# First product of the key and value compression, as four products side by side in quarters of the array's columns

## The chip, the cores and the metric

The kernel runs on one core of one Trainium2 chip. A core has five engines with their own instruction streams: TensorE (PE in the profile; PEld is its loading of weights), VectorE (DVE), ScalarE (ACT), GpSimd (POOL) and SyncE (SP, which here only starts transfers). Each engine takes its instructions in the order in which the program holds them, and waits on semaphores for what the others make. The metric is the device time of one execution in microseconds (us); lower is better.

## The reference

One decoder layer for 256 tokens of width 1024, float32 throughout. The part that matters here is the compression of the keys and values of the "native sparse attention" heads, two key/value groups of 64 columns:

```python
CMP_LEN, CMP_STRIDE, CMP_HID = 32, 16, 256

def _compress(kraw, pe, w1, b1, w2):
    B, S, G, DH = kraw.shape
    ncb = (S - CMP_LEN) // CMP_STRIDE + 1                     # 15 blocks
    idx = jnp.arange(ncb)[:, None] * CMP_STRIDE + jnp.arange(CMP_LEN)[None, :]
    blk = kraw[:, idx] + pe[None, None, :, None, :]
    blk = blk.transpose(0, 1, 3, 2, 4).reshape(B, ncb, G, CMP_LEN * DH)
    return jax.nn.gelu(blk @ w1 + b1) @ w2
```

It runs once for the keys (after their rotation) and once for the values. Each kind has 15 blocks x 2 groups = 30 rows of 32 x 64 = 2048 numbers, multiplied with a matrix of 2048 x 256 (the first product), then a GELU, then 256 x 64. The compressed keys give one of three attention branches its scores, the compressed values its output. Around it stand, in this order: a normalization modulated by a condition vector, one large projection, the retention heads and the attention heads, an output projection, a second normalization, and a retrieval of experts by product keys (PEER) with two large weight tables.

## The kernel before

The program is written in stages; a scheduler then places every engine's instructions in an order of its own, so the order in the source is not the order on an engine. Where the text below says "the order", it is the order in the built program.

Up to about 183 us runs what the source calls the prefix: the condition columns ("ada"), norm 1, the projection blocks, rotations, `compress` for keys and for values, the retention scores (`S<-qrT,krT`, copied decayed to `sT`), eight attention units, the output projection and norm 2. The rest, to 1038 us, is PEER.

`compress(kv)` does, for one kind (`"k"` or `"v"`):
- products with `ident` bring `kn` (keys) or `vcn` (values) to 64 rows a half; VectorE adds the position terms and writes `blk`, 128 rows (two tokens of a block, 64 columns each) x 16 x 30.
- four loads of 128 x 4 x 256 weights (`praw`, 0.5 MB each, three buffers, `PRAW`), and sixteen products `praw` x `blk`: the weights of the array are a 128 x 30 piece of `blk`, the moving operand 128 x 256 of `praw`. All sixteen add up in one accumulation of 30 rows x 256 in a bank `O`. Each float32 product is two records in the trace.
- ScalarE copies the sums to `hn` (30 x 256), TensorE transposes them in two parts, and a chain of small VectorE steps with one ScalarE tanh makes the GELU: `cu`, `cw` four times, `hid`.
- for the keys: `hid` x `w2k` gives the compressed keys, copied to `kcT`. For the values: `hid` x `w2v`, `vc`, a product with `rep`, and `vblk`.

`compress("k")` is called, then `compress("v")`. The scores of the attention follow: `cmp_softmax(tt)` for a half `tt` of the tokens (scores `S<-kcT,qT`, small steps `cs_s`, `cs_m`, `cs_p`, and the transposed `cs_pT`), then for each of four pairs of heads `attn_unit`: scores `S<-keys,qT`, VectorE's maximum `a_mx`, ScalarE's exponentials `a_pr` with their sums `a_sm`, a scaling, transposes `T<-ident,a_pr` and the copy `a_pT`; and `attn_pv`: products of `a_pT` with `vs` and of `cs_pT` with `vblk` into one bank `O`, a group of heads in each half of the array's columns. `mixNH` and `mixNL` are the two float32r parts of the result. Scores use two banks `S`, transposes two banks `T`.

Between these stand fillers without a part in the chain: products C of a projection block (`half`, from weights that ScalarE and VectorE split into `H` and `L`), the splits of the output projection's weights (`woH`, `woL`), and VectorE's passes over `adaraw` (128 x 1024) with which later condition columns are summed. The retention's tail (`rv`, `sg`, `rn`) ends beside the attention. Calls of helpers are all recorded at line 80.

Of the kernel before, what the change touches and what calls it, by code (L numbers as in the profile page):

```python
# [24 lines left out]
F32 = mybir.dt.float32  # L25
# [6 lines left out]
ALU = mybir.AluOpType  # L32
# [4 lines left out]
P = 128  # L37
# [11 lines left out]
PRAW = 3  # L49
# [14 lines left out]
def build(tc, I, out, dbg=None, stop=None):  # L64
# [5 lines left out]
    class Ordered:  # L70
        """An engine whose instructions stay in program order while order["on"] has its name."""
# [82 lines left out]
    def rstd_of(pool, ss, n, inv, tag):  # L154
        """1/sqrt(ss * inv + eps), a square root and one Newton step."""
# [13 lines left out]
    def rstd_pair(pool, sa, sb, tag, between=lambda: None):  # L169
        """Two factors of 1/sqrt((sa + sb) / D + eps): a square root's inverse and one Newton step."""  # L170
# [15 lines left out]
    # ------------------------------------------------------------------ prefix  # L186
# [11 lines left out]
    def table(func, dep=None):  # L198
        """Has a function's table loaded before a chain needs it, once dep is there."""
        t = mk(pers, (P, 1), F32, "tinyo", bufs=2)  # L200
        S.activation(t, tiny if dep is None else dep, func, scale=0.0)
# [29 lines left out]
    # 2 silu(c) on every partition  # L231
# [36 lines left out]
    # norm 1: the product that transposes a row block scales it too  # L268
# [38 lines left out]
    # projection blocks A (q | kc ks kw vc) and B (rq | vs vw gate)  # L307
# [92 lines left out]
    def rope(dst, src, tab, tt, nh, dh, v=0):  # L400
        """dst (SBUF) = rotated src (PSUM), nh heads of dh."""
# [24 lines left out]
    def half(c, post, nf=0):  # L426
        """A projection block of 512 columns; post(i) after each of its four units."""
# [56 lines left out]

    rr = {}
# [23 lines left out]
    # NSA transposes  # L509
# [22 lines left out]
    # compressed keys and values  # L532
# [4 lines left out]
    def compress(kv):  # L537
        pe_t, b1_t, w2_t = cmpc[kv]
# [7 lines left out]
        blk = mk(wk, (P, 16, 2, 15), F32, "blk", bufs=1)  # L546
        for s in range(2):
            rows = slice(s * 64, (s + 1) * 64)
            bv = b[rows, :].rearrange("p (g t) -> p g t", g=2)
            for g in range(2):  # L550
                src = bv[:, g, s:s + 1]
                src = bass.AP(tensor=src.tensor, offset=src.offset, ap=[list(src.ap[0]), [2, 16], [16, 15]])
                V.tensor_tensor(blk[rows, :, g, :], src, pe_t[rows, :, None].to_broadcast([64, 16, 15]), op=ALU.add)
        b = bank("O")
        for i in range(4):
            key = ("w" + kv, i)
            load(key, I["w" + kv + "1"][:, i * 4:i * 4 + 4, :], (P, 4, 256))
            r, _ = raws.pop(key)
            for q in range(4):
                mm(b[:30, :256], blk[:, i * 4 + q].rearrange("p a b -> p (a b)"), r[:, q * 256:(q + 1) * 256],  # L560
                   i == 0 and q == 0, i == 3 and q == 3)
        hn = mk(wk, (32, 256), F32, "hn", bufs=1)
        S.activation(hn[:30, :], b[:30, :256], AF.Copy)
        b = bank("O")
        for ch in range(2):
# [755 lines left out]
```

## Time and profile before

| | |
|---|---|
| time, three runs | 1039.51, 1039.74, 1041.83 us (median 1039.74) |
| span of the profiled execution | 1037.9 us (no other time of this execution is given) |
| TensorE busy over the span | 1009.2 us (97%) |
| VectorE, ScalarE, GpSimd busy | 760.4 us (73%), 606.8 us (58%), 61.5 us (6%) |
| first product of `praw` to last | 70.4 to 95.5 us |
| eight attention units | about 85 to 145 us |

The profile is one execution with the time of every instruction. A busy time counts an instruction's own time; matmul ends are modelled, and successive matmuls overlap, so their distance is read from their starts. Idle time of an engine is listed with what ended it. The rows that are used stand in a section of their own below.

### The profile page before, as it was taken

How to read it: one execution, taken by the hardware profiler on the slowest of the kernel's cores; microseconds unless marked ns; L12 is line 12 of the kernel's file. 1: busy time of each engine (PE TensorE's matmuls, PEld its weight loads, DVE VectorE, ACT ScalarE, POOL GpSimd, SP SyncE). 2: the span in 40 equal slices, each digit the busy share in tenths (PEclk: the TensorE clock that was granted, in tenths of full speed). 3: DMA queues.
4: the chain of work that ended last, by engine and by line, in shares of the span. 5: the costliest groups of instructions: out<-in, count | busy, mean ns of one | idle time of the engine just before them, and what ended most of it. 6: DMA issues, size and time to landing. Idle time of an engine off the chain costs nothing.

```text
span 1037.9 us, 17713 instructions
## 1 busy us (share of the span) xinstructions
PE 1009.2 (97%) x6580; PEld 902.1 (87%) x6582; DVE 760.4 (73%) x1653; ACT 606.8 (58%) x1244; POOL 61.5 (6%) x53
## 2 busy tenths in 40 slices
PE   7999999999998889999999999999999999999995
PEld 6876687999998889999999999988888888888884
DVE  7988888899778786667777777665955556565665
ACT  7544884555436357777777777645445555545453
POOL 1040000000331310000000000000000000000001
PEclk9999999999999999999999999999999999999998
DMA  9998753546555444444444444567976666666661
GB/s 367 352 350 335 244 181 136 168 152 183 168 149 174 144 152 135 151 147 143 148 142 144 143 143 143 156 230 231 317 234 193 197 190 214 190 199 188 198 189 57
DMA packets 56184, 199.19 MB, mean 192 GB/s; under 512 B 7305, under 2 KB 7585, under 8 KB 55713
## 3 DMA queue, kind: packets, MB, share of 16 engines
q1 hardware_dynamic: 55200, 193.59, 58.3%
q0 software_dynamic: 752, 4.20, 1.1%
q8 instruction: 51, 0.84, 0.3%
q14 instruction: 37, 0.30, 0.1%
q10 hardware_dynamic: 144, 0.26, 0.1%
HBM read 195.92 MB, written 2.11 MB: 191 GB/s over the span
## 4 chain that ended last, share of the span: by engine, by line
PE 84%; DVE 9%; POOL 3%; ACT 1%; issue 1%; DMA 0%; SPq 0%; DVEq 0%; POOLq 0%; ACTq 0%
PE acc L80 54%; PE dn L80 9%; PE w L80 7%; PE C L80 5%; PE O L80 4%; POOL oe L946 3%; PE S L80 3%; PE T L80 2%; DVE ev L80 2%; DVE L L80 2%; DVE oh L80 1%; DVE tp L80 1%; DVE VL L80 1%; DVE adaraw L80 0%; DMA xn<-in_x_dram 0%
## 5 line engine op out<-in xcount | busy, mean ns | idle before, releaser
L80 DVE TENSOR_TENSOR L<-raw,H 128x1024 fp32r<-128x1024 f32 x284 | 346.4, 1221 | 119.5 <-ACT H L80 114.9
L80 ACT ACTIVATE H<-raw 128x1024 fp32r<-128x1024 f32 x284 | 300.0, 1058 | 172.4 <-PE acc L80 132.6
L80 PE MATMUL acc<-H,a 128*128 128x512 f32 (+1 forms) x1030 | 315.9, 388 | 0.0
L80 PE MATMUL acc<-hH,H 128*128 128x256 f32 x800 | 230.8, 289 | 0.0
L80 PE MATMUL acc<-hH,L 128*128 128x256 f32 x800 | 226.6, 283 | 3.3 <-DVE L L80 3.3
L80 PEld LDWEIGHTS acc<-H,a 128*128 128x128 f32 x1030 | 193.0, 188 | 39.9
L80 PE MATMUL acc<-hL,H 128*128 128x256 f32 x800 | 226.6, 283 | 0.0
L80 PE MATMUL acc<-L,a 128*128 128x512 f32 (+1 forms) x515 | 199.7, 388 | 0.0
L80 PEld LDWEIGHTS acc<-hH,L 128*128 128x128 f32 x800 | 152.9, 191 | 4.1 <-DVE L L80 4.1
L80 PEld LDWEIGHTS acc<-hH,H 128*128 128x128 f32 x800 | 153.5, 192 | 0.1
L80 PEld LDWEIGHTS acc<-hL,H 128*128 128x128 f32 x800 | 153.2, 192 | 0.2 <-DVE hL L80 0.2
L80 PEld LDWEIGHTS acc<-L,a 128*128 128x128 f32 x515 | 96.7, 188 | 19.7
L80 ACT ACTIVATE ow<-o,VL 128x128 f16<-128x128 f16 x256 | 104.5, 578 | 5.2 <-DVE o L80 5.2
L80 PE MATMUL dn<-hH,L 128*128 128x256 f32 x352 | 99.8, 283 | 4.4 <-DVE L L80 4.4
L80 PE MATMUL dn<-hH,H 128*128 128x256 f32 x352 | 101.5, 288 | 0.4 <-ACT H L80 0.4
L80 PE MATMUL dn<-hL,H 128*128 128x256 f32 x352 | 99.6, 283 | 0.0
L80 PEld LDWEIGHTS dn<-hH,L 128*128 128x128 f32 x352 | 67.3, 191 | 5.0 <-DVE L L80 5.0
L80 PE MATMUL w<-ow,o 128*128 128x128 f16 x512 | 71.0, 296 | 0.0
L80 PEld LDWEIGHTS dn<-hH,H 128*128 128x128 f32 x352 | 67.6, 192 | 0.6 <-ACT H L80 0.6
L80 PEld LDWEIGHTS dn<-hL,H 128*128 128x128 f32 x352 | 67.4, 192 | 0.0
L80 PEld LDWEIGHTS <-o 128*128 128x128 f16 x512 | 51.9, 118 | 3.4
L80 DVE TENSOR_TENSOR ow<-o,VL 128x512 f16<-128x512 f16 x64 | 26.9, 420 | 36.9 <-PE w L80 36.9
(333 smaller groups left out, 1213.5 us busy)
## 6 DMA issues: line engine op xcount, KB each, us to landing
raw<-in_down_dram SPq DMA_DIRECT2D x128, 512.0 KB, 3.6
raw<-in_up_dram SPq DMA_DIRECT2D x128, 512.0 KB, 3.7
adaraw<-in_wadaT_dram SPq DMA_DIRECT2D x40, 512.0 KB, 8.0
raw<-in_wq_dram SPq DMA_DIRECT2D x16, 512.0 KB, 3.7
raw<-in_win_C_dram SPq DMA_DIRECT2D x12, 512.0 KB, 5.2
rawA<-in_win_A_dram SPq DMA_DIRECT2D x8, 512.0 KB, 9.6
raw<-in_wout_dram SPq DMA_DIRECT2D x8, 512.0 KB, 4.7
VL<-in_wadaT_dram SPq DMA_DIRECT2D x8, 512.0 KB, 4.6
```

The costliest lines, as they stand in the source:

```text
L80: i = fn(*a, **kw)
L946: G.tensor_tensor(oe, oh, cidx[:, p, :, None].to_broadcast([P, NCAND, 16]), op=ALU.mult)
```

## The change

The sixteen products of each kind become part of one pass for both kinds. A piece of `blk` is widened to 32 columns (two of them zero, from a memset), so that a quarter of the array's 128 columns holds it. The four quarters hold the even and the odd products of the keys and of the values; all four add up in one bank, 32 rows each. One copy of 128 x 256 takes the bank to `hn`. The even and odd sums of a kind are added when they are turned: instead of a transpose, a product with `sel4`, a 0/1 matrix that VectorE makes once from `ident`. The weights of both kinds are loaded in turn, with four buffers instead of three. Docstrings and comments are removed as well.

```diff
-PRAW = 3
+PRAW = 4
...
+    sel4 = mk(pe_, (P, 32), F32, "sel4")
+    V.tensor_reduce(sel4, ident.rearrange("p (a b) -> p b a", a=4), axis=AX.X, op=ALU.add)
...
-    def compress(kv):
-        pe_t, b1_t, w2_t = cmpc[kv]
+    def blocks(kv):
+
+        pe_t = cmpc[kv][0]
         b = bank("O")
...
-        blk = mk(wk, (P, 16, 2, 15), F32, "blk", bufs=1)
+        blk = mk(wk, (P, 16, 32), F32, "blk" + kv, bufs=1)
+        G.memset(blk, 0.0)
+        bl = blk[:, :, :30].rearrange("p a (g c) -> p a g c", g=2)
...
-                V.tensor_tensor(blk[rows, :, g, :], src, pe_t[rows, :, None].to_broadcast([64, 16, 15]), op=ALU.add)
+                V.tensor_tensor(bl[rows, :, g, :], src, pe_t[rows, :, None].to_broadcast([64, 16, 15]), op=ALU.add)
+        return blk
+
+    def compress_sums(blks):
+
         b = bank("O")
         for i in range(4):
-            key = ("w" + kv, i)
-            load(key, I["w" + kv + "1"][:, i * 4:i * 4 + 4, :], (P, 4, 256))
-            r, _ = raws.pop(key)
-            for q in range(4):
-                mm(b[:30, :256], blk[:, i * 4 + q].rearrange("p a b -> p (a b)"), r[:, q * 256:(q + 1) * 256],
-                   i == 0 and q == 0, i == 3 and q == 3)
-        hn = mk(wk, (32, 256), F32, "hn", bufs=1)
-        S.activation(hn[:30, :], b[:30, :256], AF.Copy)
+            rs = {}
+            for kv in "kv":
+                key = ("w" + kv, i)
+                load(key, I["w" + kv + "1"][:, i * 4:i * 4 + 4, :], (P, 4, 256))
+                rs[kv], _ = raws.pop(key)
+            for q2 in range(2):
+                for c, (kv, o) in enumerate((("k", 0), ("k", 1), ("v", 0), ("v", 1))):
+                    q = q2 * 2 + o
+                    PE.matmul(b[c * 32:(c + 1) * 32, :256], blks[kv][:, i * 4 + q], rs[kv][:, q * 256:(q + 1) * 256],
+                              start=i == 0 and q2 == 0, stop=i == 3 and q2 == 1, tile_position=(0, c * 32))
+        hn = mk(wk, (P, 256), F32, "hn", bufs=1)
+        S.activation(hn, b[:, :256], AF.Copy)
+        return hn
+
+    def compress(kv, hn):
+        pe_t, b1_t, w2_t = cmpc[kv]
         b = bank("O")
+        rows = slice(0, 64) if kv == "k" else slice(64, P)
         for ch in range(2):
-            PE.transpose(b[:, ch * 32:ch * 32 + 30], hn[:30, ch * P:(ch + 1) * P], ident[:30, :30])
+            mm(b[:, ch * 32:ch * 32 + 30], hn[rows, ch * P:(ch + 1) * P], sel4[rows, :30], True, True)
...
-    compress("k")
-    compress("v")
+    blks = {kv: blocks(kv) for kv in "kv"}
+    hn2 = compress_sums(blks)
+    compress("k", hn2)
+    compress("v", hn2)
```

The scheduler places the new instructions, and with them others of the prefix: on every engine the order differs from that of before up to the end of the attention and the output projection, and is the same from there on. Three places follow, each of before and then of the changed kernel, as the built programs hold them (out<-in, shape of the output; x2 is two in a row; a number is a buffer's).

TensorE, in the middle of the first sums (`O<-praw,blk`; S are retention scores, C fillers), before:

```order
L80 MATMUL O_789<-praw_790,blk_784 30x256 x3
L80 MATMUL O_789<-praw_796,blk_784 30x256 x4
L80 MATMUL O_789<-praw_802,blk_784 30x256 x4
L80 MATMUL S_913<-qrT_582,krT_583 128x256
L80 MATMUL O_789<-praw_808,blk_784 30x256 x4
L80 MATMUL S_913<-qrT_582,krT_583 128x128
L80 MATMUL S_918<-qrT_582,krT_583 128x256
L80 MATMUL O_816<-ident_66,hn_814 128x30 x2
```

and in the changed kernel, from the last load's products of both kinds to the key's `hid` and the value's turned sums:

```order
L80 MATMUL O_807<-praw_846,blkv_801 32x256 x2
L80 MATMUL O_807<-praw_844,blkk_786 32x256 x2
L80 MATMUL O_807<-praw_846,blkv_801 32x256 x2
L80 MATMUL C_1309<-H_1340,hH_144 128x512
L80 MATMUL C_1309<-L_1341,hH_144 128x512
L80 MATMUL C_1309<-H_1340,hL_145 128x512
L80 MATMUL O_858<-sel_147_624,hn_856 128x30 x2
L80 MATMUL C_1310<-H_1340,hH_144 128x512
L80 MATMUL C_1310<-L_1341,hH_144 128x512
L80 MATMUL C_1310<-H_1340,hL_145 128x512
L80 MATMUL O_872<-hid_863,w2k_616 64x15 x4
L80 MATMUL O_879<-sel_147_624,hn_856 128x30 x2
```

The retention scores have moved ahead of the last sums; between the sums and the product of `hid` there are now six C products and the two products with `sel4`.

VectorE, the key's chain from the turned sums (`cu`) to `hid`, before:

```order
L80 TENSOR_SCALAR cu_819<-O_816,b1k_614 128x30 x2
L80 TENSOR_TENSOR sT_911<-S_918,xT_909 128x256
L80 TENSOR_TENSOR cw_820<-cu_819 128x60
L80 TENSOR_TENSOR sT_210_912<-S_918,xT_909 128x128
L80 TENSOR_SCALAR cw_820<-cw_820 128x60
L80 TENSOR_TENSOR cw_820<-cw_820,cu_819 128x60
L80 TENSOR_TENSOR sT_911<-S_923,xT_909 128x256
L80 TENSOR_SCALAR cw_820<-cw_820 128x60
L80 TENSOR_TENSOR sT_210_912<-S_923,xT_909 128x128
L80 TENSOR_TENSOR hid_821<-cw_820,cu_819 128x60
L80 SCALAR_TENSOR_TENSOR adaraw_1361,acc_117<-adaraw_1361,cs_98 128x1024
```

and in the changed kernel:

```order
L80 TENSOR_SCALAR cu_861<-O_858,b1k_614 128x30 x2
L80 SCALAR_TENSOR_TENSOR adaraw_1359,acc_117<-adaraw_1359,cs_98 128x1024
L80 TENSOR_TENSOR cw_862<-cu_861 128x60
L80 TENSOR_SCALAR cw_862<-cw_862 128x60
L80 TENSOR_TENSOR cw_862<-cw_862,cu_861 128x60
L80 SCALAR_TENSOR_TENSOR adaraw_1362,acc_117<-adaraw_1362,cs_98 128x1024
L80 TENSOR_SCALAR cw_862<-cw_862 128x60
L80 TENSOR_TENSOR hid_863<-cw_862,cu_861 128x60
```

The four copies to `sT` have left the chain, and two passes over `adaraw` stand in it.

ScalarE, around the last attention unit (its scaling `a_pr<-a_pr,a_sm` and its copies `a_pT`), before:

```order
L80 ACTIVATE woH_388_1631<-raw_1629 128x1024
L80 ACTIVATE a_pr_1269<-a_pr_1269,a_sm_1260 128x256 x2
L80 ACTIVATE a_pr_1272<-a_pr_1272,a_sm_1260 128x256 x2
L80 ACTIVATE a_pT_1284<-T_1279 128x512
L80 ACT_TABLE_LOAD
L80 ACTIVATE rys_1442<-ryv_1440 128x4
L80 ACTIVATE a_pT_1293<-T_1288 128x512
L80 ACTIVATE woH_392_1640<-raw_1638 128x1024
L80 ACTIVATE woH_396_1649<-raw_1647 128x1024
L80 ACTIVATE mixNH_905<-O_1120 128x4x128
```

and in the changed kernel:

```order
L80 ACT_TABLE_LOAD
L80 ACTIVATE rys_1443<-ryv_1441 128x4
L80 ACTIVATE woH_391_1641<-raw_1639 128x1024
L80 ACT_TABLE_LOAD
L80 ACTIVATE sg_1583<-C_1497 128x512
L80 ACTIVATE a_pr_1270<-a_pr_1270,a_sm_1261 128x256 x2
L80 ACTIVATE a_pr_1273<-a_pr_1273,a_sm_1261 128x256 x2
L80 ACTIVATE a_pT_1285<-T_1280 128x512
L80 ACTIVATE a_pT_1294<-T_1289 128x512
L80 ACTIVATE sg_1594<-C_1498 128x512
L80 ACTIVATE woH_395_1650<-raw_1648 128x1024
L80 ACTIVATE mixNH_906<-O_1121 128x4x128
```

Two table loads, a `woH` and the first `sg` now stand ahead of the last unit's scaling.

## Rows read from the trace of the kernel before

**Rows 1.** Busy time by stage: window, us, then each engine's busy (instructions), clock, DMA.

```profile
60.00:65.00 5.00, 5.00 (x23) 4.14 (x23) 4.96 (x11) 1.07 (x3) 4.57 (x4) 1.00 0.89 311
70.30:87.40 17.10, 17.10 (x100) 10.34 (x99) 14.37 (x35) 5.36 (x12) 0.31 (x1) 1.00 1.03 404
87.70:143.30 55.60, 55.37 (x331) 36.28 (x331) 47.00 (x117) 44.03 (x133) 0.00 (x0) 1.00 0.72 247
143.30:160.00 16.70, 16.45 (x113) 14.09 (x112) 14.66 (x37) 12.32 (x18) 0.00 (x0) 1.00 0.43 133
```

**Rows 2.** The weights' tile, then the timeline of TensorE (start, us, instruction, count).

```profile
L80 PE MATMUL O<-praw,blk x64: 379/379/402, 70.4 to 95.5; 128*30 128x256 f32 x64
...
87.08 0.40 PE L80 MATMUL C<-L,hH 128*128 128x512 f32 x1
87.40 5.37 PE L80 MATMUL O<-praw,blk 128*30 128x256 f32 x24
```

**Rows 3.** Timeline of TensorE, products into halves of the columns.

```profile
122.81 0.98 PE L80 MATMUL O<-a_pT,vs 128*64 128x128 f32 x13
123.53 0.27 PE L80 MATMUL O<-cs_pT,vblk 128*64 128x128 f32 x1
123.63 0.27 PE L80 MATMUL O<-a_pT,vs 128*64 128x128 f32 x1
```

**Rows 4.** Timelines of ScalarE, VectorE and TensorE along the key's chain.

```profile
78.94 0.37 ACT L80 ACTIVATE hn<-O 30x256 f32<-30x256 f32 x1 [5.26 <-PE O L80]
...
80.45 0.42 DVE L80 TENSOR_TENSOR sT<-S,xT 128x256 f32<-128x256 f32 x1
80.92 0.28 DVE L80 TENSOR_TENSOR sT<-S,xT 128x128 f32<-128x128 f32 x1
82.81 1.22 DVE L80 SCALAR_TENSOR_TENSOR adaraw<-adaraw,cs 128x1024 f32<-128x1024 f32 x1
83.95 0.08 DVE L80 DVE_READ_ACCUMULATOR adaraw<-adaraw,cs 128x1 f32 x1
...
83.05 0.42 PE L80 MATMUL O<-hid,w2k 128*64 128x15 f32 x8
87.77 0.37 ACT L80 ACTIVATE a_pr<-S,a_mx 128x128 f32<-128x128 f32 x1 [2.80 <-DVE a_mx L80]
```

**Rows 5.** ScalarE's groups, 87.7 to 143.3: count, busy, mean ns, idle before.

```profile
L80 ACT ACTIVATE H<-raw 128x1024 fp32r<-128x1024 f32 x5 | 5.3, 1060 | 2.3 <-PE C L80 2.2
L80 ACT ACT_TABLE_LOAD x1 | 1.3, 1283 | 0.0
L80 ACT ACTIVATE hn<-O 30x256 f32<-30x256 f32 x1 | 0.4, 373 | 3.8 <-PE O L80 3.8
```

**Rows 6.** Timelines at the attention's end: ScalarE, TensorE, VectorE.

```profile
142.63 0.58 ACT L80 ACTIVATE a_pT<-T 128x512 f32<-128x512 f32 x1
145.16 0.60 ACT L80 ACTIVATE mixNH<-O 128x512 fp32r<-128x512 f32 x1
143.82 0.98 PE L80 MATMUL O<-a_pT,vs 128*64 128x128 f32 x13
159.18 0.63 PE L80 MATMUL T<-ident,rn 128*128 128x128 f32 x4 [0.25 <-DVE rn L80]
146.79 1.21 DVE L80 TENSOR_TENSOR woL<-raw,woH 128x1024 fp32r<-128x1024 f32 x1
```

**Rows 7.** SyncE's timeline, the key's fourth load; then all `praw` loads to landing.

```profile
66.84 0.33 SPq L80 DMA_DIRECT2D praw<-in_wk_dram  x1
...
DMA to landing us min/median/max: 6.1/8.4/9.3
```

**Rows 8.** Windows around the one stretch early in the kernel with a low clock.

```profile
7.00:10.40 3.40, 1.23 (x11) 1.17 (x11) 2.86 (x9) 2.40 (x6) 0.68 (x1) 1.00 1.03 419
10.40:13.90 3.50, 3.50 (x19) 3.50 (x19) 3.39 (x9) 2.77 (x5) 0.00 (x0) 0.51 1.03 418
```

**Rows 9.** TensorE's waits over the whole run: for what, total us, times, longest.

```profile
PE dn L80 <- DVE L L80: 4.4, 3, 2.6
```

## The prediction

> **What bounds the kernel now.** I read the windows by stage first [rows 1]. TensorE is busy for all 17.10 us of the stretch in which the compression of the keys runs, for 55.37 of the 55.60 us of the attention and for 16.45 of 16.70 us behind it, so in this kernel the end is set by the sum of its work. ScalarE is busy for 44.03 of the 55.60 us: it has 11.6 us of slack there, no more. Then the products that the change touches [rows 2]: 64 records of `praw`, all on 30 columns; 24 of them take 5.37 us including the modelled end of the last (0.38), so their pitch is (5.37 - 0.38)/23 = 0.217 us. A filler product of 512 columns costs 0.23: 22 of them fill the 5.00 us from 60 on, where the row counts 23 with the parts at the edges [rows 1]. Third, rows of products that go to the two halves of the columns [rows 3]. Fourth, the chain from a kind's sums to the first exponential [rows 4]. Fifth, ScalarE's groups in the attention with their idle time [rows 5], then the end of the attention [rows 6]. The order of the instructions after the attention stage's tail is the same in both kernels, so what is gained or lost up to there shifts all the rest. The profiled span is 1037.9 us; the median of the runs is 1039.74, 1.8 above it, and I carry the difference over.
>
> **The sums themselves.** Removed: 64 x 0.217 = 13.9 us of TensorE. Added: the same 64 records, spread over four column groups. The order has them in runs of 2, 14, 2, 6, 2 and 6 products with S and C products between; in the fullest quarter that is a chain of 1 + 4 + 1 + 2 + 1 + 2 = 11 products of two records, 11 x 0.434 = 4.8 us. That needs four at a time. What the trace shows is two at a time: thirteen records of 128 columns start within 0.72 us, 0.055 each [rows 3], where 128 columns of a lone record take 0.217/2 = 0.108. It also shows how: a record of `cs_pT` starts between the two records of the `a_pT` product ahead of it, so a product for free columns doesn't wait for the second record of the one before. Nothing in that is special to two groups, so I take four (4.8) and keep two (32 x 0.217 = 6.9) as the other end. Sums by products with `sel4` instead of transposes add some 0.25 us, changes between column patterns 0.2 (the first sum starts 0.32 behind a C product that costs 0.23: at most 0.09 for each of some eleven, perhaps nothing). TensorE's work falls by 13.9 - 4.8 - 0.45 = 8.7 us.
>
> The Trainium skill ("TensorE: Matmul & The Clock Gate", Part 3, The mechanism) says that matrix products start in strict program order, without reordering. Taken record by record, that rule speaks against four at a time: the second record of each product would hold up the next, and two would run together, which by the rule makes 6.9 us instead of 4.8. The `cs_pT` row above speaks against this reading.
>
> **The weights' transfers.** All eight now arrive for one pass. The last four stand behind one another where the fourth load of the key kind stood, issued at 66.84 [rows 7]; with at most 9.3 us to landing the first of the four is there by 76.1, and the others follow at some 1.3 us (0.52 MB at 404 GB/s [rows 1]), the last by 80. By the order, the first is needed near 78.5 and the last near 83.5: hidden, with 2 us of cover; without it each us late would be a us of TensorE. The other new steps: two memsets of 128x512 at the front of POOL's queue, at most 1.2 us if they take what ScalarE's copy of that size takes [rows 6], tens of us before the blocks are filled; and one reduction of `ident` on VectorE among the ropes, between nothing and the 0.42 us of a step on 256 elements [rows 4]. Both 0. The value kind's transposes and blocks move ahead of the sums: the same work, but the sums start near 72 instead of 70.4.
>
> **The chain behind the sums.** Here a wait is added. Before, the copy `hn` starts at 78.94 and the product of `hid` at 83.05, 4.1 us later [rows 4], while TensorE has scores and C products to do. After, the sums end later: start 72, chain 4.8, seventeen C products between (3.9), the scores of four heads (2.6: 0.65 each by the same pitch) and about 0.8 for the pattern changes and a wait for `krT`: 84.2. Then the same chain without the four sT copies (2 x 0.42 + 2 x 0.28 = 1.4), but with two passes of `adaraw` inside it, 1.14 each on VectorE [rows 4]: 4.1 - 1.4 + 2.3 = 5.0, so `hid` is multiplied at about 89.2. TensorE has only six C products and one `sel4` pair to put there (1.6 us): it stands still some 3.1 us, and behind this product, in order, stand the value's `sel4` pair, the compressed scores and the first scores of every head. From `hid` to the first exponential it is 4.7 us before; the same again, a little less because the value's transposes are gone from between, puts it at 93.8 instead of 87.77: **6 us later**. Further on TensorE waits, by the order, for two score banks that the first exponentials still hold (1.7 and 0.5) and for `cs_p` (0.8); a part of the 3.0 closes if ScalarE is quick, and I count 2.0. Of the 8.7 us, 8.7 - 3.1 - 2.0 = 3.6 are left at best, in the form of C products done ahead of time.
>
> **ScalarE takes the pace.** Up to the last `a_pT` (ends 143.2 [rows 6]) ScalarE does 43.8 us of work before (the 44.03 without 0.2 of a copy that begins behind it). After, `hn` (0.37) and two smaller activations (0.6 together) have left this stretch; one table load (1.28), one `sg` (0.6, as a copy of 512 columns [rows 6]) and one more `woH` (1.06, as an H copy) now stand ahead of the last unit's `a_pT` [rows 5]. 43.8 - 1.0 + 2.9 = 45.7 us. From 93.8 that ends at 139.5 plus ScalarE's idle time. Before, it is idle for 11.6 us: 3.8 before `hn`, which goes; 2.2 of the 2.3 before H copies are waits for C products [rows 5], which TensorE now has done earlier; 5.6 are others. Following the order with these durations I find 1.8 us of waits that it forces; with the 5.6 as the other end I take 2.8, nearer to the forced ones, because TensorE is ahead. The last `a_pT` then ends near **142.3** (141.3 to 145.1).
>
> **The tail.** Before, TensorE takes up the last product with `a_pT` 0.6 us after it is there (143.82 [rows 6]) and is busy nearly without a break to the second transpose of `rn` at 159.18. After, it starts at once (-0.6) and has seven C products fewer to do (-1.6). But right behind the last unit now stands a product with `mixNH`, and ScalarE has `sg` and a `woH` (1.7) to do first, then `mixNH` itself (0.60): TensorE waits 1.1. Behind the transposes stands a product with a `woL` that VectorE splits only after two others (1.21 each), `mixNL`, `rn` and the statistics: another 1.9. Together 3.0 - 2.2 - 0.25 (a wait of before that goes) = +0.5, with some 0.3 of that made up in the order of the last C products: +0.2. So the kernel is even if the last `a_pT` ends near 143.0, that is with 3.5 us of idle time on ScalarE; at 142.3 it gains 0.7. Forecast: **1039.74 - 0.7 = 1039.0**, and with the ends of the idle time 1038.0 to 1041.8. About 0.3% (3.1 us) is what a measurement of this kernel can tell from no change.
>
> **The rivals.**
> *TensorE stays the bound.* If ScalarE catches up (idle under 1 us) and the tail's two waits close because `sg` and the splits come earlier, the 3.6 us stay: 1036.1. For it: 11.6 us of idle time before. Against: 2.9 us of new ScalarE work just before the last unit.
> *ScalarE keeps its waits (the slower case).* One mechanism: VectorE's `adaraw` passes and `L` splits stand ahead of the reciprocals that the scaling waits for, so that ScalarE's idle time other than `hn`'s stays whole: 11.6 - 3.8 = 7.8. The last `a_pT` ends at 147.3, 4.3 late: 1044.0; with 5.6 it is 1041.8. It decides from 3.5 us on. For it: VectorE is busy 47.00 of 55.60 us [rows 1].
> *Only two products at a time.* The change then doesn't do what it says: 6.9 - 4.8 = 2.1 us later at the first exponential: 1041.1.
> *The clock.* TensorE's granted clock was 0.51, the 1.2 GHz level, from 10.4 to 13.9 us, after it had been busy 1.23 of 3.40 us [rows 8]; a wait of 2.6 us for a down weight later left it at the upper level, 2.4 GHz [rows 9]. The new stall of 3.1 us with small products behind it lies between. At the lower level for one such stretch, about 1.75 us of work more, all ahead of the first exponentials: 1040.8.
>
> **How the numbers follow.** Forecast 0.46, TensorE bound 0.19, ScalarE's waits 0.16, two at a time 0.09, the clock 0.10. The range reaches to the TensorE case below and, above, to the ScalarE case with 6 us of idle time: 1036.0 to 1042.3; outside lie half of that case's upper part and some of the TensorE case, under 0.2 together. Faster by over 0.3% (under 1036.6): most of the TensorE case and a little of the forecast, 0.19. Slower by over 0.3% (over 1042.9): the ScalarE case from 6.7 us of idle time on and the combinations with it, 0.18. Within 0.3%: 0.63.
>
> **What would show it.** Right: starts of four `praw` records within some hundredths of a us and about 4.8 us of TensorE for them all; sums ending near 84; a wait of TensorE for `hid` near 3 us; the first `a_pr` near 94; then ScalarE busy over 90% up to a last `a_pT` near 142.3; waits for `mixNH` and a `woL` behind it. Wrong: records of one pair starting after the pair before (two at a time); a granted clock near 0.5 around 90; a first `a_pr` before 92, which would mean that the order's two `adaraw` passes cost less; ScalarE idle over 4 us after 94, which is the slower case; or any time that comes from behind 184 us, where the order is the same and I expect nothing.

## The result: 0.7% slower, and what the profile after shows

The changed kernel takes **1047.64 us** (median; 1046.78 to 1048.06), the kernel before 1039.74: a ratio of 1.0070, 95% interval 1.0058 to 1.0083. The forecast was 1039.0, the range ended at 1042.3. Executions of one kernel fall into two groups some 1.3 us apart (the kernel before mostly at 1039.5 to 1040.0 or at 1040.7 to 1041.8), so a median alone can move by that much. The profiled span grew from 1037.9 to 1045.1. The first product of the next stage (`acc<-hH,H`) starts at 189.74 us, and at 183.15 before: 6.6 of the 7.2 us are lost ahead of it.

TensorE's timeline after (start, us, instruction, records, in brackets the idle time before it and what ended it):

```profile
73.77 0.41 PE L80 MATMUL O<-praw,blkv 128*32 128x256 f32 x2
73.78 0.41 PE L80 MATMUL O<-praw,blkk 128*32 128x256 f32 x2
74.01 0.39 PE L80 MATMUL O<-praw,blkv 128*32 128x256 f32 x2
...
84.64 0.60 PE L80 MATMUL O<-praw,blkv 128*32 128x256 f32 x4
...
90.49 0.52 PE L80 MATMUL O<-hid,w2k 128*64 128x15 f32 x8 [2.92 <-issue]
...
189.74 0.74 PE L80 MATMUL acc<-hH,H 128*128 128x256 f32 x4
```

The sums do what the change says. Four records start within 0.02 us and the next four 0.24 later, where one record alone had a pitch of 0.217 [rows 2]. The last sums end at 85.2. Then TensorE finishes its few C products and stands still for 2.92 us until `hid` is there. Before, it had no wait here.

The windows around that wait (us; busy time of PE, PEld, DVE, ACT, POOL with instructions; granted clock, DMA share, GB/s):

```profile
87.40:90.40 3.00, 0.18 (x1) 0.00 (x0) 2.89 (x9) 0.25 (x1) 0.00 (x0) 1.00 0.33 72
90.40:92.00 1.60, 1.51 (x13) 1.44 (x13) 0.00 (x0) 0.91 (x3) 0.00 (x0) 0.58 1.00 399
92.00:96.00 4.00, 4.00 (x13) 2.69 (x13) 1.48 (x8) 0.95 (x3) 0.00 (x0) 0.50 0.50 187
96.00:98.00 2.00, 2.00 (x5) 0.80 (x4) 1.33 (x6) 1.09 (x7) 0.00 (x0) 0.63 0.00 0
98.00:148.00 50.00, 47.92 (x289) 31.49 (x288) 45.62 (x106) 44.15 (x127) 0.00 (x0) 1.00 0.73 264
148.00:152.00 4.00, 3.79 (x23) 3.02 (x24) 2.79 (x9) 3.01 (x5) 0.00 (x0) 0.59 0.31 123
```

Behind the wait the granted clock is 0.50, the lower level of 1.2 GHz, for almost seven us. "PE busy" is full from 92 to 96, but with 13 instructions: they are slow, not many. A second such stretch lies at 148 to 152.

ScalarE and VectorE after, from the sums to the last attention unit:

```profile
85.28 0.38 ACT L80 ACTIVATE hn<-O 128x256 f32<-128x256 f32 x1 [11.29 <-PE O L80]
87.05 1.21 DVE L80 SCALAR_TENSOR_TENSOR adaraw<-adaraw,cs 128x1024 f32<-128x1024 f32 x1
88.80 1.22 DVE L80 SCALAR_TENSOR_TENSOR adaraw<-adaraw,cs 128x1024 f32<-128x1024 f32 x1
90.17 0.22 DVE L80 TENSOR_TENSOR hid<-cw,cu 128x60 f32<-128x60 f32 x1
96.91 0.37 ACT L80 ACTIVATE a_pr<-S,a_mx 128x128 f32<-128x128 f32 x1 [1.46 <-DVE a_mx L80]
...
145.71 1.70 ACT L80 ACTIVATE a_pr<-a_pr,a_sm 128x256 f32<-128x256 f32 x4
147.31 1.22 ACT L80 ACTIVATE a_pT<-T 128x512 f32<-128x512 f32 x2
```

`hn` starts at 85.28 (78.94 before), the product of `hid` at 90.49 (83.05), the first exponential at 96.91 (87.77 [rows 4]): 9.1 us late. The attention from there to the end of the last `a_pT` takes 51.6 us (55.4 before), and from there to the next stage it is 41.2 (39.9 before). TensorE's longest waits from 45 to 200 us (what for; sum, times, longest):

```profile
PE O L80 <- issue: 2.9, 1, 2.9
...
PE S L80 <- DVE mixRL L80: 1.9, 1, 1.9
PE T L80 <- ACT a_pr L80: 1.6, 1, 1.6
```

In the 51.6 us of the attention TensorE is busy for 49.4 and waits twice, 0.40 us for an `H` and the 1.64 for `a_pr`. ScalarE is busy for 45.8 and idle for 5.9 us, more than half of it ahead of its copies `a_pT`, for TensorE's transposes (count, busy us, mean ns, idle before):

```profile
L80 ACT ACTIVATE a_pr<-a_pr,a_sm 128x256 f32<-128x256 f32 x16 | 6.8, 504 | 0.7 <-DVE a_sm L80 0.7
L80 ACT ACTIVATE a_pr<-a_pr,a_sm 128x128 f32<-128x128 f32 x16 | 5.1, 394 | 0.9 <-DVE a_sm L80 0.9
L80 ACT ACTIVATE a_pT<-T 128x512 f32<-128x512 f32 x8 | 4.6, 596 | 0.6 <-PE T L80 0.5
L80 ACT ACTIVATE a_pT<-T 128x256 f32<-128x256 f32 x8 | 3.1, 382 | 2.7 <-PE T L80 2.6
```

### The profile page after: what moved, and what is told of

It is laid out like the page before. It is cut to its first block, busy times and chain, and to the rows that moved or that the text cites. A ratio compares the mean times of both kernels' runs of the same rounds, so it can differ in the third digit from the quotient of the medians.

```text
span 1045.1 us, 17720 instructions
## 1 busy us (share of the span) xinstructions
PE 1010.3 (97%) x6586; PEld 903.2 (86%) x6586; DVE 761.1 (73%) x1654; ACT 604.5 (58%) x1243; POOL 61.6 (6%) x55
## 4 chain that ended last, share of the span: by engine, by line
PE 83%; DVE 10%; POOL 4%; ACT 2%; issue 1%; DMA 0%; SPq 0%; DVEq 0%; POOLq 0%; ACTq 0%
PE acc L80 54%; PE dn L80 9%; PE w L80 7%; PE C L80 4%; PE O L80 3%; POOL oe L966 3%; PE S L80 3%; DVE L L80 2%; DVE ev L80 2%; PE T L80 2%; DVE adaraw L80 1%; DVE oh L80 1%; DVE tp L80 1%; DVE woL L80 1%; DVE VL L80 1%
```

## The experiments

In most of them the issue order of one of the two kernels is held: each engine's order up to the end of the prefix is given to the scheduler as a table, so that an edit moves what it names and nothing else. First exponential, end of the last `a_pT` and start of the next stage are those of each kernel's profiled execution, which can lie up to 2 us from the median (warm_key's took 1046.09, half_sums' 1036.44, best_after's 1042.43, best_k4's 1042.28). Each ratio compares with executions of the kernel before taken beside that run (their medians go from 1039.74 to 1040.94), so it says more than the difference of two medians in the table.

| kernel | median, us | ratio to before (95%) | first exp. | last `a_pT` ends | next stage |
|---|---|---|---|---|---|
| before | 1039.74 | | 87.77 | 143.21 | 183.15 |
| changed | 1047.64 | 1.0070 (1.0058 to 1.0083) | 96.91 | 148.53 | 189.74 |
| warm_key | 1044.15 | 1.0039 (1.0025 to 1.0053) | 95.08 | 145.95 | 188.72 |
| late_ada | 1045.30 | 1.0047 (1.0030 to 1.0064) | 94.54 | 145.48 | 188.26 |
| tail_order | 1047.40 | 1.0075 (1.0058 to 1.0092) | 97.00 | 147.17 | 190.24 |
| short_ada | 1046.98 | 1.0071 (1.0054 to 1.0088) | 96.90 | 148.57 | 188.69 |
| best_after | 1043.73 | 1.0038 (1.0024 to 1.0052) | 92.81 | 142.05 | 184.71 |
| best_k4 | 1040.92 | 1.0005 (0.9996 to 1.0015) | 92.77 | 142.00 | 185.01 |
| before_chain | 1044.78 | 1.0043 (1.0027 to 1.0060) | 93.21 | 148.56 | 188.49 |
| chain_warm | 1042.66 | 1.0018 (1.0008 to 1.0028) | 90.28 | 145.39 | 185.99 |
| half_sums | 1037.76 | 0.9972 (0.9960 to 0.9983) | 86.10 | 139.95 | 179.89 |
| per_kind | 1038.79 | 0.9985 (0.9975 to 0.9994) | 90.17 | 139.39 | 180.61 |
| kind_chain | 1036.14 | 0.9965 (0.9954 to 0.9977) | 87.28 | 138.35 | 179.01 |

### The clock and the chain, in the changed kernel

**warm_key**, the stall filled:

```diff
+            warm = [PE.matmul(b[:, 128:256], ident, ident, start=True, stop=True) for _ in range(12)]
             # then the products with hid, as before
```

> The changed kernel with its issue order held on every engine, and twelve products of ident with itself (their result is not read) put on TensorE ahead of the first product with hid, into the 2.92 us in which TensorE stands still there (12 x 0.215 = 2.6 us). Theory 1, the clock: TensorE fell to 0.50 from 90.8 to 97.25 because it stood still, and small products followed. Then here the granted clock stays at 1.0 through 88 to 98 us, hid is multiplied where it was (90.5), the first exponential comes some 1.8 us earlier (95.1 instead of 96.9), and the first down product some 1.8 earlier than 189.7: about 1045.8 us instead of 1047.6. Theory 2, the order behind: ScalarE's waits and the table load ahead of the last unit set the end of the attention whatever comes before; then the first exponential moves by 1.8 and the end by under 0.5: 1047.2 to 1047.6. If the clock stays at 0.50 all the same, the stall is not its cause.

```profile
90.00:93.00 3.00, 2.81 (x29) 2.55 (x29) 1.50 (x6) 1.31 (x3) 0.00 (x0) 1.00 0.04 3
93.00:97.00 4.00, 3.95 (x18) 1.97 (x19) 3.71 (x13) 2.47 (x14) 0.00 (x0) 1.00 0.96 311
```

These windows of warm_key have the clock at 1.00. Its timelines:

```profile
91.18 0.42 PE L80 MATMUL O<-hid,w2k 128*64 128x15 f32 x8 [0.20 <-DVE hid L80]
95.08 0.37 ACT L80 ACTIVATE a_pr<-S,a_mx 128x128 f32<-128x128 f32 x1 [0.33 <-DVE a_mx L80]
```

From the product of `hid` to the first exponential it is 3.90 us, and 6.42 in the changed kernel: **the lower clock cost 2.5 us**. The median falls by 3.5; between the two profiled executions (1046.84 and 1046.09) the first exponential comes 1.8 us earlier and the next stage 1.0, as `hn` comes 0.7 later here. The idle TensorE, with small products behind it, was the cause; how `hid` came about is unchanged (5.2 us behind `hn` in both). In the tail stretches at the lower clock remain (0.67 from 144 to 148, 0.50 from 156 to 159).

**late_ada**, the two `adaraw` passes out of the chain (VectorE's order):

```diff
 cu<-O,b1k x2
-adaraw,acc<-adaraw,cs 128x1024
 cw<-cu ... cw<-cw,cu
-adaraw,acc<-adaraw,cs 128x1024
 cw<-cw
 hid<-cw,cu
+adaraw,acc<-adaraw,cs 128x1024 x2
```

> The changed kernel with its issue order held on every engine, but for the two adaraw passes on VectorE (1.14 us each) that stood inside the chain from hn to hid: they are put right behind hid. Theory 1, chain and clock: hid comes 2.3 us earlier (87.9 instead of 90.2), TensorE's stall falls from 2.9 to about 0.6 us, the clock then stays at 1.0, and the first exponential comes 2.3 + 1.8 = 4.1 us earlier (92.8 instead of 96.9); at most all of it is kept to the end: 1043.5 us, and at least half: 1045.6. If the clock falls all the same, 2.3 of it: 1045.3. Theory 2, the order behind: under 1 us is kept, 1046.7 or more, with ScalarE's idle time between its first and last attention instruction grown by what the start gained.

Its timelines:

```profile
89.21 0.42 PE L80 MATMUL O<-hid,w2k 128*64 128x15 f32 x8 [1.11 <-DVE hid L80]
94.54 0.37 ACT L80 ACTIVATE a_pr<-S,a_mx 128x128 f32<-128x128 f32 x1 [1.32 <-DVE a_mx L80]
```

and its window behind the wait:

```profile
90.00:93.00 3.00, 3.00 (x12) 1.89 (x12) 2.74 (x12) 1.33 (x4) 0.00 (x0) 0.62 0.61 174
```

The chain shrank by 1.8 us, and 2.3 us of time are won. A wait of 1.11 us was enough for the clock to fall here; so the first exponential gained 2.4 and not 4.1.

### The same cause put into the kernel before

**before_chain** (VectorE's order in the kernel before):

```diff
-adaraw,acc<-adaraw,cs 128x1024
 sT<-S,xT ... cu ... cw
+adaraw,acc<-adaraw,cs 128x1024 x2
 hid<-cw,cu
-adaraw,acc<-adaraw,cs 128x1024
```

> The kernel before with its issue order held, but two adaraw passes on VectorE (1.14 us each) moved into the keys' chain, directly ahead of the step that makes hid: one from behind it and one from ahead of the chain. VectorE's work is the same; only the keys' hid comes 2.3 us later (85.0 instead of 82.7). It puts what is suspected in the changed kernel into the kernel before, without any other part of the change. If a late keys' chain costs by itself (TensorE has no work in its order to put there), TensorE waits some 2.2 us, and the end comes 2.3 to 4 us later, 1042 to 1043.9 us, more where the clock falls as well. If the kernel before, which has 11.6 us of idle time on ScalarE, absorbs it: 1039.4 to 1041.

Its timelines, and the windows behind the wait and in the attention:

```profile
85.51 0.42 PE L80 MATMUL O<-hid,w2k 128*64 128x15 f32 x8 [2.12 <-DVE hid L80]
93.21 0.37 ACT L80 ACTIVATE a_pr<-S,a_mx 128x128 f32<-128x128 f32 x1 [5.78 <-DVE a_mx L80]
188.49 0.74 PE L80 MATMUL acc<-hH,H 128*128 128x256 f32 x4
```

```profile
84.00:90.00 6.00, 4.49 (x34) 4.06 (x35) 3.73 (x12) 1.41 (x3) 0.00 (x0) 0.67 1.03 405
90.00:93.00 3.00, 3.00 (x5) 1.18 (x5) 0.51 (x1) 0.00 (x0) 0.00 (x0) 0.51 1.03 399
98.00:136.00 38.00, 37.94 (x236) 24.50 (x235) 31.88 (x77) 30.33 (x98) 0.31 (x1) 1.00 0.69 231
```

The product of `hid` is 2.5 us late, the first exponential 5.4, the next stage 5.3. ScalarE's idle time absorbed **nothing**: the attention takes 55.4 us from its first exponential, as before. TensorE is busy for 55.29 us of these (37.94 of 38.00 in the window above), so its own work is enough to explain that; whether ScalarE could have made up time behind a TensorE with less to do, this run doesn't ask. **chain_warm** adds nine idle products (the edit of warm_key, with 9) to that:

> The kernel of the run before_chain (the kernel before with the keys' hid 2.3 us later), and nine products of ident with itself on TensorE ahead of the product with hid (their result is not read), which fill 1.95 of the 2.12 us of the new wait. In before_chain the granted clock was 0.5 from 86 to 93 us and the first exponential came 5.4 us late, of which 2.3 are the delay. If the other 3.1 are the clock's, it stays at 1.0 here, the first exponential comes at 90 to 90.5 instead of 93.2, the first product of the next stage at 185.4 to 186 instead of 188.5, and the time is 1041.7 to 1042.5 us. If they come from waits that follow from the delay (exponentials that hold score banks, VectorE's order), little changes: 1044 to 1045.

```profile
90.28 0.37 ACT L80 ACTIVATE a_pr<-S,a_mx 128x128 f32<-128x128 f32 x1 [2.81 <-DVE a_mx L80]
185.99 1.20 PE L80 MATMUL acc<-hH,H 128*128 128x256 f32 x4
```

```profile
84.00:90.00 6.00, 5.89 (x53) 4.48 (x53) 4.21 (x13) 1.41 (x3) 0.00 (x0) 1.00 1.03 404
90.00:93.00 3.00, 3.00 (x15) 1.49 (x16) 3.00 (x8) 1.82 (x9) 0.00 (x0) 1.00 1.04 402
```

The clock stays up, and what remains is the delay alone: the first exponential is 2.5 us late, the next stage 2.8, the time 1042.66 (by its ratio 0.8 to 2.9 us above the kernel before). In the kernel before, too, the lower clock costs 2.9 us at the first exponential, and a late chain costs its lateness in full at the next stage of these two executions.

### The tail

**tail_order** holds the changed kernel's order and moves one `sg`, with its table load, behind the last two `a_pT` copies on ScalarE:

```diff
-sg<-C 128x512   (and its table load)
 a_pr<-a_pr,a_sm x4
 a_pT<-T 128x512 x2
+sg<-C 128x512   (and its table load)
```

> The changed kernel with its issue order held on every engine, but for one instruction on ScalarE: the first sg, and with it the table load of 1.28 us that it needs, goes from ahead of the last attention unit's scaling to behind that unit's two a_pT copies. Theory of ScalarE's order (the prediction's slower rival, ScalarE held up at the end): the scaling starts at about 143.9, when VectorE has a_sm, instead of 145.71; TensorE's wait of 1.64 us ahead of the last transposes goes, and with it the second stretch at the lower clock (148 to 152.5): the first down product comes 2 to 3.3 us earlier than 189.74, about 1044.3 to 1045.6 us. Theory of VectorE (its passes, held up from 72 to 98, pile up behind 136 and set when rn and mixRL are there): under 1 us is gained, 1046.7 or more, and TensorE's wait moves to rn or mixRL.

Its timeline on TensorE:

```profile
150.56 1.22 PE L80 MATMUL C<-woH,mixNH 128*128 128x512 f32 x2 [2.03 <-ACT woH L80]
...
158.49 0.50 PE L80 MATMUL C<-woL,mixNH 128*128 128x512 f32 x1 [1.65 <-DVE woL L80]
```

The wait of 1.64 us for `a_pr` is gone and the last `a_pT` ends 1.4 us earlier, but TensorE now waits 2.03 us for `woH` in its place: 1047.40, no gain. Moving this one instruction only moves the wait, and the new one is for ScalarE again, so its order as a whole isn't ruled out. Up to the last `a_pT` TensorE now has no wait at all, and the attention still takes 50.2 us.

**short_ada** asks whether VectorE's total does, by shortening eight `adaraw` passes:

```diff
+        n = 256 if 24 <= j < 32 else D
-        V.scalar_tensor_tensor(w, w, 0.5, cs, ...)
+        V.scalar_tensor_tensor(w[:, :n], w[:, :n], 0.5, cs[:, :n], ...)
```

> The changed kernel with its issue order held, but the eight adaraw passes that VectorE runs between 133 and 148 us read 256 columns instead of 1024, which leaves out three quarters of each sum: some 8 x 0.85 = 6.8 us of VectorE less at the end of the attention. Theory of VectorE: its backlog there holds up a_sm, the woL splits, rn and mixRL; the waits for them (1.89 for mixRL, part of the 1.64 ahead of the last transposes) go, 2 to 4 us: 1043.6 to 1045.6. Theory of ScalarE's order: ScalarE is busy without a gap from 138.5 to 149.9 and issues the table loads and sg ahead of the scaling whatever VectorE does: under 1 us, 1046.7 or more.

1046.98: nothing that can be measured, though the next stage starts at 188.69 instead of 189.74. The waits stay (for `woL` 2.1, for `a_pr` 1.6); the clock is at 1.00 from 148 to 152 here (0.59 in the changed kernel), which may be the one us. So shorter passes of VectorE alone gain nothing either. By its time each of the two runs came out as the other engine's theory had it: with one engine's part taken away, the other's wait is still there.

**best_after** joins what had helped: the `adaraw` passes out of the chain (late_ada), five idle products in the stall, `sg` behind `a_pT`.

> The changed kernel with its issue order held and three edits at once: the two adaraw passes behind hid, the first sg behind the last a_pT copies, and five idle products of ident on TensorE ahead of hid (their result is not read), which fill the 1.11 us that is left of the stall. If the causes found so far (chain, clock, ScalarE's order at the end) add up, about 2.3 + 1 + 2 to 3 of the 7.9 us are made good: 1041 to 1042.5, with no stretch at the lower clock between 85 and 160. If they share one bound behind them (VectorE's backlog), it is no better than the best of them alone, 1044.

Its timeline on TensorE:

```profile
145.44 0.73 PE L80 MATMUL C<-woH,mixNH 128*128 128x512 f32 x2 [2.03 <-ACT woH L80]
...
153.00 0.50 PE L80 MATMUL C<-woL,mixNH 128*128 128x512 f32 x1 [2.55 <-DVE woL L80]
...
184.71 0.74 PE L80 MATMUL acc<-hH,H 128*128 128x256 f32 x4
```

The first exponential is at 92.81, and the attention now takes 49.2 us to the last `a_pT` (142.05, where the forecast had 142.3), with TensorE busy for 48.3 of them and the clock at 1.00 from 86 to 164. The time, 1043.73, is above the 1041 to 1042.5 expected: the next stage comes at 184.71, 1.6 us later than before, since the tail takes 42.7 us, two waits in it. The `woL` waited for is the split that TensorE multiplies first and that VectorE makes last. **best_k4** moves only this one on VectorE:

```diff
 rn,sg ...
+woL (396)
 woL (400)
 woL (404)
-woL (396)
```

> The kernel of the run best_after, and one instruction more moved on VectorE: the split woL of the fourth block of the output weights, which TensorE multiplies first but VectorE splits only behind those of the fifth and sixth block, two statistics and mixRL, goes ahead of those (directly behind the first product of rn with sg). In best_after TensorE waits 2.55 us for a woL there, up to 153.0. Theory of the tail's order: what is left of the loss (184.71 at the first product of the next stage, against 183.15 in the kernel before) is this wait; then it falls to under 0.5, and the product of the next stage starts at 182.2 to 183.3: 1041.2 to 1042.4 us. If VectorE's or ScalarE's total sets that point, another wait takes its place: 184.2 or more, 1043.2 to 1043.9 us.

```profile
PE C L80 <- ACT woH L80: 2.0, 1, 2.0
...
PE C L80 <- DVE woL L80: 0.2, 1, 0.2
```

The 2.55 us wait is 0.24 now and the time falls by 2.8 to 1040.92: level with the kernel before (1.0005, 0.9996 to 1.0015). So with the `adaraw` passes out of its chain, the stall filled and the longest wait of its tail gone the changed kernel gains nothing. Its profiled execution, which took 1042.28, shows the lower clock once more (mean 0.84 and 0.73):

```profile
144.00:148.00 4.00, 2.61 (x16) 2.52 (x17) 4.00 (x11) 3.72 (x5) 0.00 (x0) 0.84 0.00 0
148.00:152.00 4.00, 4.00 (x26) 3.96 (x26) 4.00 (x7) 2.25 (x4) 0.00 (x0) 0.73 0.40 128
```

so its start of the next stage (185.01) isn't that of its median.

### What cheaper sums are worth, and the change done one kind at a time

**half_sums** holds the order of the kernel before and leaves out every second product of the sums:

```diff
-            for q in range(4):
+            for q in (0, 2):
```

> The kernel before with its issue order held on every engine, and every second product of the compression's first product left out on both kinds (32 of 64 records, 32 x 0.217 = 6.9 us of TensorE); the transfers stay. It leaves out half of the contraction. It asks what less work there is worth where the order around it is the one of the kernel before. If TensorE's work sets the end and ScalarE has slack, as the prediction's first part says, most of 6.9 us is gained: 1033 to 1035.5 us. If the chain behind the sums and ScalarE take the pace at once, as the prediction's last part says of the change, 3.45 us are gained at the first exponential (87.8 - 3.5 = 84.3) and 0 to 3 at the end: 1036.7 to 1039.7.

```profile
75.90 1.05 PE L80 MATMUL O<-praw,blk 128*30 128x256 f32 x4 [0.96 <-DMA praw<-in_wk_dram]
...
179.89 0.76 PE L80 MATMUL acc<-hH,H 128*128 128x256 f32 x4
```

Of the 6.9 us of TensorE's work that went (32 x 0.217 [rows 2]), 3.3 are kept at the next stage and 1.8 to 4.2 in the time (0.9972, 0.9960 to 0.9983). A part goes to new waits: 0.96 us for a weight load that had been hidden, and 2.14 for `cs_p` at 92.89. Even where the chain starts earlier (1.7 us at the first exponential), less than half of the saved sums is kept at the next stage.

**per_kind** takes the four quarters for one kind at a time, keys first, as in the kernel before, with three load buffers. All products of a load are then one kind's four quarters:

```diff
 def compress_sums(kv, blk):
+    for q in range(4):
+        PE.matmul(b[q*32:(q+1)*32, :256], blk[:, i*4+q], r[:, q*256:(q+1)*256],
+                  start=i == 0, stop=i == 3, tile_position=(0, q*32))
...
+    for kv in "kv":
+        compress(kv, compress_sums(kv, blocks(kv)))
```

> The sums side by side in four column quarters, but one kind at a time, the keys first, as the kernel before has it: sixteen products of a kind in the four quarters, each quarter a fourth of the contraction, three weight buffers. It undoes the loading of both kinds together; its order around the sums is its own: twelve C products stand between the sums of hn and the product with hid, and the value kind's sums behind the keys' scores. Theory 1 (what costs is that the keys' chain starts only when both kinds' sums are done, and then finds TensorE without work): the sums of the keys take 1.75 us, no stall of over 1 us before hid, clock at 1.0, first exponential 4 to 6 us ahead of the kernel before (82 to 84), and most of the 8.7 us of TensorE's saved work kept: 1031 to 1036 us. Theory 2 (ScalarE and the order of the attention are the bound, whatever the sums take): first exponential as early, ScalarE idle more behind it, 1038 to 1041 us.

```profile
74.07 1.50 PE L80 MATMUL O<-praw,blkk 128*32 128x256 f32 x22
...
85.56 0.42 PE L80 MATMUL O<-hid,w2k 128*64 128x15 f32 x8 [0.91 <-issue]
```

```profile
90.17 0.37 ACT L80 ACTIVATE a_pr<-S,a_mx 128x128 f32<-128x128 f32 x1 [1.25 <-DVE a_mx L80]
```

1038.79 (0.9985): the scheduler, left to itself, put two `adaraw` passes into the chain here too, at 81.77 and 83.04, and the first exponential is 2.4 us later than before, where 82 to 84 was expected. Cheaper sums did not start the chain earlier: `hn` starts at 80.17 here (78.94 before), since the sums start later (73.15, 70.37 before) and retention scores and C products, 4.0 us of them, stand ahead of the keys' last eight records. **kind_chain** holds per_kind's order and moves `adaraw` passes on VectorE:

```diff
-adaraw,acc<-adaraw,cs 128x1024 x3   (among cu, cw, hid and the first a_mx)
 hid<-cw,cu
+adaraw,acc<-adaraw,cs 128x1024
 a_mx<-S
+adaraw,acc<-adaraw,cs 128x1024 x2
```

> The kernel of the run per_kind with its issue order held, but for three adaraw passes on VectorE: the two that stood inside the keys' chain from hn to hid go behind it, one right behind hid and the other, with the pass that stood there, behind the first a_mx. If the start of ScalarE's attention work sets the end, as the runs so far say, the first exponential comes about 2 us earlier than 90.17 and 1 to 2 us are kept: 1036.8 to 1037.8. If VectorE's total is the bound there (25.6 of the 28 us from 70 to 98 busy), moving passes gains nothing at the end: 1038.3 to 1039.3.

```profile
83.01 0.42 PE L80 MATMUL O<-hid,w2k 128*64 128x15 f32 x8
...
179.01 0.74 PE L80 MATMUL acc<-hH,H 128*128 128x256 f32 x4
```

```profile
87.28 0.37 ACT L80 ACTIVATE a_pr<-S,a_mx 128x128 f32<-128x128 f32 x1 [2.34 <-DVE a_mx L80]
```

The first exponential is 2.9 us earlier than in per_kind, the next stage 1.6, the median 2.65. **1036.14 us, ratio 0.9965 (0.9954 to 0.9977): faster than both kernels.** The product of `hid` is where it was before (83.05 [rows 4]), without a wait, and the first exponential 0.5 us earlier; from there to the last `a_pT` it takes 51.1 us instead of 55.4, and the next stage starts 4.1 us earlier. In the attention TensorE is busy for 48.6 us (55.2 before): the values' sums, four at a time, are a part of that. In best_k4 the attention is shorter still (49.2), but its first exponential comes 5.0 us later than before and its tail is 3.1 us longer (43.0, a part at the lower clock), which takes the gain.

## Why the prediction was wrong, step by step

**The sums: right.** Four at a time, about 5.5 us for all of them against 4.8 and 0.2 of changes; the weights' transfers hidden. They end at 85.2 instead of 84.2. The rival of two at a time is refuted, and with it the reading, record by record, that the prediction set against four. The Trainium skill ("TensorE: Matmul & The Clock Gate", Part 3, The mechanism) says further, in its list of what overlaps, that a load of weights overlaps running products only where the row groups differ; its text lets a load run ahead into a background weight buffer, too. The trace differs from the list: the four products share all 128 rows, differ only in columns, and run together (four in 0.24 us), and the loads for the next four start at 73.80 us, while these four, started from 73.77 on, still run (the next start at 74.01).

**The chain to `hid`: right.** 5.2 us from `hn` to its product (forecast 5.0), a stall of 2.92 us (3.1; the prediction's own terms, 5.0 less 1.6 us of work, give 3.4).

**From `hid` to the first exponential: the first failed step.** The forecast took "the same again", at most 4.7 us; it was 6.42, because the clock fell. This was the rival priced at 1.75 us with a chance of 0.10. It came about, and warm_key puts 2.5 us on it, the pair before_chain and chain_warm 2.9. The row I leaned on, a wait of 2.6 us that left the clock up [rows 9], was no guide: the clock also fell after waits of 2.1 and 1.1 us. With the sums' 1.1 us and the chain's 0.2 the first exponential is at 96.9 instead of 93.8.

**"ScalarE takes the pace": the second, and the largest.** I let ScalarE set the end of the attention, with 11.6 us of slack to make up for a late start: 2.8 us of idle time were to be left. The traces show TensorE in that place, where the prediction's first paragraph had put it for the kernel before. In that kernel, with the start 5.4 and 2.5 us late (before_chain, chain_warm), the attention takes 55.4 and 55.1 us, TensorE is busy for 55.29 and 55.05 of them, and ScalarE's idle time is not used up: in before_chain 6.3 us of it are waits for TensorE's sums and C products (6.0 before [rows 5]). In the changed kernel TensorE is busy for 49.4 of 51.6 us, and in tail_order, without a wait, the attention still takes 50.2 (its first 2 us at the lower clock). ScalarE's work there is what I added up (45.77, forecast 45.7); its idle time is 5.9 us and not 2.8, a little beyond my upper end of 5.6. The size is that of the slower rival. Its mechanism, VectorE ahead of the scalings, can account for 1.6 us of the 5.9 (the idle time that ends with `a_sm`), TensorE's transposes for 3.2; no run removed VectorE's passes from the whole attention. That best_after comes near the forecast, 49.2 and 48.5, is luck: TensorE is busy for 48.3 us of it, a sum that I didn't make.

**The tail: the third.** From the last `a_pT` on +0.2 us were forecast; it is +1.3 (41.2 against 39.9). Of the two waits that I priced, the 1.1 us for `mixNH` isn't there. The other, 1.9 us ahead of a product with `woL`, comes as 1.89, one group earlier in TensorE's order (that `woL` is ready at 157.85). What I had at nothing is the clock: its second stretch at the lower level lies in the tail, from 148.7 to 152.1 us. In short_ada, with the same attention and the clock at 1.00 there, the tail is 40.1 us, as forecast, but VectorE also had less to do. In best_after, with an earlier end of the attention and the clock at 1.00, it is 42.7, with waits of 2.03 for `woH` and 2.55 for `woL`.

**The sum.** At the next stage, 189.74 came instead of 182.45 (the forecast's 183.15 - 0.7): 7.3 us, of which 3.1 lie ahead of the first exponential (1.1 in the sums, 0.2 in the chain, 1.8 behind `hid`), 3.1 in the attention and 1.1 in the tail. No rival alone reaches 1047.6 (the slower one ends at 1044.0); the clock, priced at 1.75 us and 0.10, came together with an idle time of ScalarE at the lower end of the slower rival's. How much of the tail's 1.1 us is the clock's isn't cleanly separable.

**What stays open.** Behind the start of the next stage the changed kernel takes another 0.6 us (1045.1 - 189.74 = 855.4, and 854.75 before), where I forecast nothing; half_sums, before_chain and chain_warm have 854.5 to 855.1, the variants of the changed kernel 855.4 to 855.6. I haven't traced it. The wait of 1.89 us that the profile after puts down to `mixRL` stands in front of a product that doesn't read it; what it waits for isn't settled, but the product behind it would have waited for its `woL` up to 157.85 all the same. And in the tail the same wait didn't always bring the clock down: 1.64 us did in the changed kernel (0.59) and not in short_ada (1.00), 2.03 us did in tail_order (0.80) and not in best_after; what makes the difference isn't shown by these runs.

## What to carry to other kernels

Price a saving by what it does to the chain that starts the next stage: merging a kind that this chain needs with one that can wait delayed it. Where TensorE had work without a break behind it, the delay was paid in full whatever idle time ScalarE showed (5.4 us gave 5.3 at the next stage, 2.5 gave 2.8); in three other pairs a little over half of a shift of the first exponential arrived there (1.0 of 1.8 in warm_key, 1.5 of 2.4 in late_ada, 1.6 of 2.9 from per_kind to kind_chain). Done for the needed kind first, with the helper passes out of its chain, the same edit won 0.35%. Where a change makes TensorE stand still ahead of small products, price the lower clock as well, or give it idle products to do. In a list of splits, make first what is multiplied first.

## What the runs showed of the hardware that was not expected

Four FP32 products side by side in quarters of the columns cost what one costs: four records per 0.24 us at the start (in per_kind 22 records in six such starts take 1.50 us, thus (1.50 - 0.38)/5 = 0.22 from start to start), where a lone record's pitch is 0.217 [rows 2]. The loads of their weights start within 0.02 us of one another (73.77 to 73.79 us), those for the next four at once behind them.

A short wait can cost about as much again: after 2.92, 2.12 and 1.11 us without work, with products of 15 columns next, the mean granted clock was 0.50 to 0.67 for some 3 to 7 us; after the first two 2.5 and 2.9 us were lost by it. Nine or twelve products with nothing to compute (five behind the shorter chain of best_after) kept it at 1.00. It isn't so after every such wait: 2.03 and 2.55 us in best_after left the clock up.
